# A convolution's running sum moved into a PSUM bank, and two score tiles that share three banks

## The chip, the cores and the metric

The kernel runs on one core of a Trainium2 chip. Time is device microseconds (us) of one execution; the number that counts is the median of three runs. One further execution was recorded by the hardware profiler, and all rows below come from it. PE is the matrix engine (its weight loads are listed as PEld), DVE the vector engine, ACT the scalar engine, POOL the third elementwise engine, SP the engine that issues transfers. SBUF is the working memory. PSUM is the accumulator memory that PE writes to: 8 banks of 512 fp32 columns on each of 128 partitions.

## What is computed

Two transformer-like blocks follow each other, each of two layers, on 512 tokens of width 1024. The change touches only the second block's mixer. It has three branches whose results are concatenated: a Fourier mix, a latent attention of 8 heads, and a depthwise convolution of 31 taps over 256 channels. In the first layer of the block a context of 256 tokens goes through the same mixer; in the second layer only the 512 tokens do, while attention still reads all 768 keys.

```python
def conformer_conv(zg, w_dw, b_dw, ln_g, ln_b, w_pw2):
    a, g = jnp.split(zg, 2, axis=-1)
    u = a * jax.nn.sigmoid(g)
    u = lax.conv_general_dilated(u, w_dw[:, None, :], ...) + b_dw     # 31 taps
    u = jax.nn.silu(layer_norm(u, ln_g, ln_b))
    return u @ w_pw2

def mla_attend(qn, qr, kn, kr, v):
    s = jnp.einsum("bqhd,bkhd->bhqk", qn, kn) + jnp.einsum("bqhr,bkr->bhqk", qr, kr)
    p = jax.nn.softmax(s.astype(jnp.float32) * ATTN_SCALE, axis=-1).astype(v.dtype)
    return jnp.einsum("bhqk,bkhd->bqhd", p, v)
```

## The kernel before

Every product is made of three matmuls (high times high, high times low, low times high part), so that each operand exists as a rounded copy (written by ACT) and a remainder (written by DVE or POOL).

The program is not issued in the order in which the code is written. The functions record operations through proxies, all on line 489 of the kernel, which is why every row of the profile names that line. `Sched.run` then orders them: it steps through a planned time with a cost for each operation (`_cost`) and a flag for operations of DVE and POOL that may not run side by side (`_port`), takes on each engine the ready operation that stands first in priority, and gives out buffers by tag. A tag is a set of slots; an operation that needs a slot waits in the plan until one is free. The instructions are issued in the planned order, each engine works through its own in that order, and semaphores are set between them by a layer below that sees which instruction touches which tile.

The two mixers of the second block are one phase each, `m20` and `m21` in the code. `B2` says how the eight banks are used there: `sc2` holds attention scores, two tiles of 1024 columns, which is four banks; the other four banks are single tiles for everything else. A block of scores has 128 queries by 768 keys, or by 256 keys where the context attends to itself, so a block fills half to three quarters of such a tile.

In `attend` each block of scores is made by a group of matmuls (nine of 256 columns for 768 keys, three for 256), then DVE takes the row minimum (`tensor_reduce`), and ACT the exponential with its sum (`activation`, followed by a small read of the accumulator). PE transposes the exponentials, ACT and DVE split them, PE multiplies them with the values. With 8 heads the first layer has 32 blocks of 768 keys and 16 of 256, the second 32 of 768.

The convolution runs beside all this, as filling. `taps(i, b)` does one block of 128 channels (b) of one stream (i: the tokens or the context). Of the 31 taps 25 run on DVE, as a chain in which each takes the shifted input `cu`, multiplies it with a column of `half` and adds the running sum `a`, a tile of tag `h` in SBUF. The other six (`BESIDE`) are products made by ACT and POOL and summed by POOL into `c`; a last addition of POOL joins the two. `conv_rest` does the normalisation and the closing matmuls. `conv` lays the two channel blocks side by side, one tap of each at a step; `tick` and the loop over `fills` decide how many steps have been recorded by which point of the other work.

Of the kernel before, what the change touches and what calls it, by code (L numbers as in the profile page):

```python
# [12 lines left out]
F32 = mybir.dt.float32  # L13
# [3 lines left out]
ALU = mybir.AluOpType  # L17
AX = mybir.AxisListType

P = 128  # L20
# [23 lines left out]
MIX = 0.5  # L44
WAIT = 1.0
MARGIN = 100
TICK = 3
FREE = 0.2
DMA = 2.0
FSTEP = (20, 18)  # L50
CSTEP = (48, 32)
B2 = {"sc2": 2, "mm tr acc ms": 4}
BESIDE = 6
TAPS = 'AP'
NEARLY = 4
# [470 lines left out]


def _in_psum(x):
    return isinstance(x, View) and x.buf.tag in ("mm", "tr", "acc", "ms", "sc", "sc2")


def _port(eng, name, out, ins):
# [33 lines left out]
def kernel(  # L566
# [30 lines left out]
    sc = Sched(tc)  # L597
    TE, V, S, G, SP = (sc.proxy(e) for e in ("PE", "DVE", "ACT", "POOL", "SP"))
# [22 lines left out]
    def psum(tag="mm", n=T):  # L621
        return sc.alloc(banks.get(tag, tag), n)
# [710 lines left out]
    def mixer2(l, mp, ux, uc):  # L1333
        last = l == L - 1
        NK = T + TC
        SX, SC = (ux[0], ux[1], T), (uc[0], uc[1], TC)
        both = [SX] if last else [SX, SC]
# [33 lines left out]
        def taps(i, b):  # L1371

            u, n, first = convs[i][b], both[i][2], 31 - BESIDE
            a = accs[n, b] = sc.alloc("h", n)
            c = sc.alloc("h", n)
            done = 0
            for j in range(first):
                if j == 0:
                    V.tensor_scalar(out=a, in0=u[:, 0:n], scalar1=wdw(b * 31), scalar2=col(f"bdw{l}", b), op0=ALU.mult, op1=ALU.add)
                else:  # L1380
                    V.scalar_tensor_tensor(out=a, in0=u[:, j:j + n], scalar=wdw(b * 31 + j), in1=a, op0=ALU.mult, op1=ALU.add)
                while done * first < (j + 1) * BESIDE:
                    k = first + done
                    q = t32(n) if done else c
                    if TAPS[done % len(TAPS)] == "A":
                        S.activation(q, u[:, k:k + n], AF.Copy, scale=wdw(b * 31 + k))
                    else:
                        G.tensor_scalar(out=q, in0=u[:, k:k + n], scalar1=wdw(b * 31 + k), scalar2=0.0, op0=ALU.mult, op1=ALU.add)
                    if done:
                        G.tensor_tensor(out=c, in0=c, in1=q, op=ALU.add)  # L1390
                    done += 1
                yield
            G.tensor_tensor(out=a, in0=a, in1=c, op=ALU.add)

        def conv_rest(acc, n):
            xs = [out_split(acc[b], n) for b in range(2)]
# [72 lines left out]
        def fourier(ams):  # L1469

            for s, am in reversed(list(zip(both, ams))):
                n = s[2]
                parity = n // TC
                yf[n] = [operand(n) for f in range(2)]
                for p in range(parity):
                    w = wload(dft_d[(0 if n == T else 2) + p])
                    ps = psum()
                    for f in range(2):
                        o = slice(f * TC, f * TC + TC)
                        for t in range(4):  # L1480
                            x = am[p * 2 + t // 2]
                            a = slice(t % 2 * 256 + f * P, t % 2 * 256 + f * P + P)
                            c = slice(t * TC, t * TC + TC)
                            mm3(ps[:, o], x[0][:, a], x[1][:, a], w[0][:, c], w[1][:, c], t == 0, t == 3)
                        split(*(x.rearrange("p (j b) -> p b j", b=parity)[:, p] for x in yf[n][f]), ps[:, o])
                        yield
# [83 lines left out]
        def block_taps(b):  # L1570
            for i in range(len(both)):
                yield from taps(i, b)

        def conv():
            yield from zip_longest(block_taps(0), block_taps(1))
            for s in both:
                yield from conv_rest([accs[s[2], b] for b in range(2)], s[2])

        convs, yf, yc, accs = [[] for _ in both], {}, {}, {}
        cv, ticks = conv(), [0]  # L1580
# [145 lines left out]
                    v = values(1)  # L1726

        steps = main()
        fills = [(fourier(ams), 4 if last else 6, FSTEP[l]), (cv, (31 - BESIDE + 4) * len(both) - ticks[0], CSTEP[l])]
        done = [0, 0]  # L1730
        for i, _ in enumerate(steps, 1):
            for x, (f, n, span) in enumerate(fills):
# [9 lines left out]
    @contextmanager  # L1742
    def phase(name, shares, slots=()):

        with ExitStack() as st:
            p = pool(name, None, st)
            pp = pool(name + "p", bass.MemoryType.PSUM, st)
            banks.clear()
            sc.here = [tags.split()[0] for tags in shares]
            for tags, n in shares.items():  # L1750
                tag = tags.split()[0]
                banks.update((x, tag) for x in tags.split())
                if tag == "sc2":
                    sc.slots(pp, tag, n, 1024, F32)
                    banks["sc"] = "sc2"
                else:
                    sc.slots(pp, tag, n, 512, F32)
            for tag, n, cols, dt in slots:
                sc.slots(p, tag, n, cols, dt, tag in ("r", "t"))
            yield p  # L1760
            for tag, n in SPARE.get(name[:2], {}).items():
                sc.tags[tag].spare = n
            sc.run()
            sc.drop_extra()
# [264 lines left out]
```

## Time and profile before

| | us |
|---|---|
| median of three runs | 3466.51 (3465.47 to 3468.73) |
| the profiled execution | 3464.11 |
| its span, first to last instruction | 3462.3 |
| PE busy | 3366.1 (97% of the span) |
| DVE busy | 2293.6 (66%) |
| ACT busy | 1458.9 (42%) |
| POOL busy | 795.3 (23%) |

The shares are means over stages that differ. The mixer of the second block's first layer lies at about 1900 to 2200 us of the span, that of the second layer at about 2820 to 3060. In each, projections come first, and then a stretch of attention: from the first score matmul to the last group of them it goes from 2020.70 to 2176.80 in the first layer and from 2931.00 to 3030.70 in the second. A matmul is listed with some 280 ns although one of 256 columns follows the next after about 117 ns, because matmuls overlap; so PE's busy time counts the tail of the last one before a gap as well. In the rows of groups an instruction's mean duration stands in ns behind the busy time, and the idle time before it at the end.

### The profile page before, as it was taken

To read this page: it belongs to the slowest core of one execution; us is meant where nothing else is said; L and a number is where in the kernel's file an instruction comes from. 1 tells how busy PE (TensorE), PEld (TensorE's weight loads), DVE (VectorE), ACT (ScalarE), POOL (GpSimd) and SP (SyncE) were. 2 spreads that over 40 slices of the span, in tenths; PEclk is the share of its full clock that TensorE was granted. 3 is DMA by queue.
4 is the path that set the end of the run, shared out by engine and by line. 5 is a ranking of instruction groups with operands and counts; after the bars stand their busy time and mean duration, and the time that the engine had idled before them with its cause. 6 is when DMAs were issued, how large, how long until landed. Compare 5 with 4: busy or idle time off the path is not lost.

```text
span 3462.3 us, 48309 instructions
## 1 busy us (share of the span) xinstructions
PE 3366.1 (97%) x18565; PEld 2901.3 (84%) x18565; DVE 2293.6 (66%) x4092; ACT 1458.9 (42%) x2751; POOL 795.3 (23%) x710
## 2 busy tenths in 40 slices
PE   8999999999999999999999988999999998999999
PEld 8888888888888888888888876898888887888888
DVE  8888875865388788658654998564443369963334
ACT  5555444322355554443223376441221244843223
POOL 3112323111131032231112443120110235320002
PEclk9999999999999999999999999999999999999999
DMA  3222223543332212236533110223332221123332
GB/s 126 64 71 67 74 67 134 191 168 127 106 101 65 71 61 80 73 134 195 176 128 116 46 37 7 98 80 112 109 109 92 68 81 48 32 79 98 97 96 81
DMA packets 100744, 326.14 MB, mean 94 GB/s; under 512 B 11168, under 2 KB 18336, under 8 KB 100512
## 3 DMA queue, kind: packets, MB, share of 16 engines
q1 hardware_dynamic: 100512, 323.05, 29.0%
q8 instruction: 145, 2.38, 0.3%
q14 instruction: 87, 0.71, 0.1%
HBM read 313.57 MB, written 9.44 MB: 93 GB/s over the span
## 4 chain that ended last, share of the span: by engine, by line
PE 84%; DVE 10%; ACT 3%; issue 2%; POOL 1%; DMA 0%; SPq 0%; DVEq 0%; ACTq 0%; POOLq 0%
PE mm L489 78%; PE sc L489 4%; DVE r L489 3%; DVE h L489 2%; DVE s L489 2%; PE acc L489 2%; DVE t L489 1%; ACT r L489 1%; DVE w L489 1%; ACT e L489 1%; ACT t L489 0%; DMA raw<-in_win_dram 0%; ACT w L489 0%; POOL t L489 0%; POOL x L489 0%
## 5 line engine op out<-in xcount | busy, mean ns | idle before, releaser
L489 PE MATMUL mm<-r,w 128*128 128x512 f32 (+2 forms) x12044 | 2521.2, 360 | 17.7 <-DVE w L489 7.5
L489 PEld LDWEIGHTS mm<-r,w 128*128 128x128 f32 (+1 forms) x12044 | 2009.0, 189 | 347.6 <-DVE w L489 11.0
L489 DVE TENSOR_TENSOR w<-raw,w 128x1024 fp32r<-128x1024 f32 (+2 forms) x466 | 588.2, 1270 | 639.6 <-issue 327.8
L489 ACT ACTIVATE w<-raw 128x1024 fp32r<-128x1024 f32 (+1 forms) x466 | 483.5, 1047 | 1035.1 <-PE mm L489 946.8
L489 ACT ACTIVATE e<-sc,s 128x512 f32<-128x512 f32 (+2 forms) x208 | 153.4, 740 | 99.6 <-DVE s L489 94.7
L489 POOL TENSOR_TENSOR x<-t,x 128x512 fp32r<-128x512 f32 (+1 forms) x58 | 83.0, 1434 | 409.1 <-ACT x L489 397.5
L489 PE MATMUL mm<-rc,w 128*128 128x256 f32 x768 | 166.1, 281 | 0.0
L489 PEld LDWEIGHTS mm<-rc,w 128*128 128x128 f32 x768 | 139.8, 189 | 20.2
L489 DVE TENSOR_REDUCE s<-sc 128x1 f32<-128x512 f32 (+2 forms) x208 | 151.4, 741 | 7.6 <-PE sc L489 7.1
L489 POOL TENSOR_TENSOR t<-t,t 128x512 f32<-128x512 f32 (+2 forms) x70 | 89.0, 1273 | 237.5 <-DVE t L489 200.3
L489 PE MATMUL mm<-r,r 128*128 128x256 f32 (+1 forms) x588 | 118.8, 333 | 8.1 <-DVE r L489 6.8
L489 ACT ACTIVATE t<-mm 128x512 f32<-128x512 f32 (+4 forms) x126 | 68.0, 540 | 135.0 <-PE mm L489 129.9
L489 DVE SCALAR_TENSOR_TENSOR h<-cu,half,h 128x512 f32<-128x512 f32 (+1 forms) x144 | 116.4, 819 | 0.5
L489 PE MATMUL mm<-sums 128*128 128x256 f32 x757 | 107.2, 291 | 9.7 <-DVE sums L489 6.4
L489 DVE TENSOR_TENSOR r<-mm,r 128x256 fp32r<-128x256 f32 (+1 forms) x266 | 105.6, 433 | 14.3 <-ACT r L489 12.4
L489 ACT ACTIVATE r<-mm 128x256 fp32r<-128x256 f32 (+1 forms) x272 | 94.8, 401 | 44.5 <-PE mm L489 41.3
L489 PEld LDWEIGHTS mm<-sums 128*128 128x128 f32 x757 | 101.2, 198 | 13.2 <-DVE sums L489 6.6
L489 ACT ACTIVATE r<-t 128x512 fp32r<-128x512 f32 (+3 forms) x141 | 83.1, 597 | 68.8 <-DVE t L489 55.9
L489 PEld LDWEIGHTS mm<-r,r 128*128 128x128 f32 x588 | 90.8, 193 | 23.4 <-DVE r L489 8.4
L489 DVE TENSOR_TENSOR r<-t,r 128x512 fp32r<-128x512 f32 (+2 forms) x134 | 105.4, 794 | 7.5 <-ACT r L489 6.3
L489 PE MATMUL mm<-w,r 128*128 128x256 f32 x704 | 102.4, 285 | 4.9 <-DVE w L489 3.1
L489 PEld LDWEIGHTS mm<-w,r 128*128 128x128 f32 x704 | 91.5, 190 | 7.4 <-DVE w L489 3.5
(636 smaller groups left out, 4358.8 us busy)
## 6 DMA issues: line engine op xcount, KB each, us to landing
raw<-in_wm_dram SPq DMA_DIRECT2D x256, 512.0 KB, 3.5
raw<-in_win_dram SPq DMA_DIRECT2D x134, 512.0 KB, 3.6
mraw<-in_wmod_dram SPq DMA_DIRECT2D x64, 512.0 KB, 4.4
raw<-in_wmod_dram SPq DMA_DIRECT2D x32, 512.0 KB, 3.5
raw<-in_wbr_dram SPq DMA_DIRECT2D x24, 512.0 KB, 3.5
raw<-in_wout_dram SPq DMA_DIRECT2D x16, 512.0 KB, 4.0
raw<-in_wo_dram SPq DMA_DIRECT2D x16, 512.0 KB, 3.5
kept<-h SPq DMA_DIRECT2D x24, 256.0 KB, 3.2
```

Source lines behind the costliest of these rows:

```text
L489: getattr(self.engines[eng], name)(*[_real(x) for x in a], **{n: _real(x) for n, x in k.items()})
```

## The change

The running sum of the DVE taps lies in a PSUM bank of its own (tag `cv`, one slot) in place of SBUF; the bank is named as PSUM to the planner, which then no longer takes these taps for operations that keep POOL waiting. The last addition of a chain goes from POOL to DVE, from PSUM and SBUF to a tile of tag `h`. To free the bank, the two score tiles have 768 columns each and are cut from one tile of 1536 columns, three banks; the first covers the first bank and half of the second, the other the rest. Since there is one slot for a running sum, the channel blocks are done one behind the other. A step is now one tap, so the number of steps is doubled in `TICK` and in `fills`.

```diff
-TICK = 3
+TICK = 6
...
-B2 = {"sc2": 2, "mm tr acc ms": 4}
+B2 = {"sc2": 2, "mm tr acc ms": 4, "cv": 1}
...
-    return isinstance(x, View) and x.buf.tag in ("mm", "tr", "acc", "ms", "sc", "sc2")
+    return isinstance(x, View) and x.buf.tag in ("mm", "tr", "acc", "ms", "sc", "sc2", "cv")
...
             u, n, first = convs[i][b], both[i][2], 31 - BESIDE
-            a = accs[n, b] = sc.alloc("h", n)
-            c = sc.alloc("h", n)
+            a, c = psum("cv", n), sc.alloc("h", n)
...
-            G.tensor_tensor(out=a, in0=a, in1=c, op=ALU.add)
+            accs[n, b] = sc.alloc("h", n)
+            V.tensor_tensor(out=accs[n, b], in0=c, in1=a, op=ALU.add)
...
         def conv():
-            yield from zip_longest(block_taps(0), block_taps(1))
+            for b in range(2):
+                yield from block_taps(b)
...
-        fills = [(fourier(ams), 4 if last else 6, FSTEP[l]), (cv, (31 - BESIDE + 4) * len(both) - ticks[0], CSTEP[l])]
+        fills = [(fourier(ams), 4 if last else 6, FSTEP[l]), (cv, (2 * (31 - BESIDE) + 4) * len(both) - ticks[0], CSTEP[l])]
...
                 if tag == "sc2":
-                    sc.slots(pp, tag, n, 1024, F32)
+                    t = pp.tile([P, n * 768], F32, tag=tag, name=tag)
+                    sc.tags[tag] = Tag([t[:, i * 768:(i + 1) * 768] for i in range(n)], 0)
```

DVE, first layer, start of the convolution, before. `cu5120` and `cu5121` are the padded inputs of the two channel blocks of the tokens, `cu2560` that of the context, `h5` and `h1` running sums, `w` and `raw` weights.

```order
L489 SCALAR_TENSOR_TENSOR h5_144<-cu5120_14461,half_14465,h5_144 128x512 [waits DVE_49] x2
L489 TENSOR_TENSOR w0_102<-raw0_108,w2_104 128x1024 [waits DMAHW2_49,PE_49,Activation_49]
L489 SCALAR_TENSOR_TENSOR cu2560_14463<-t5_120,mm0_14453 128x256
L489 TENSOR_TENSOR w5_107<-raw2_110,w5_107 128x8x32 [waits DMAHW4_49,Activation_49]
L489 SCALAR_TENSOR_TENSOR h5_144<-cu5120_14461,half_14465,h5_144 128x512 [waits DVE_49]
L489 TENSOR_SCALAR h1_140<-cu2560_14463,half_14465,vec_148 128x256 [waits DVE_49]
L489 SCALAR_TENSOR_TENSOR h5_144<-cu5120_14461,half_14465,h5_144 128x512 [waits DVE_49]
L489 TENSOR_TENSOR w3_105<-raw1_109,w4_106 128x1024 [waits DMAHW3_49,PE_49]
L489 SCALAR_TENSOR_TENSOR h5_144<-cu5120_14461,half_14465,h5_144 128x512 [waits DVE_49] x6
```

The same place in the changed kernel; `cv0` is the running sum in PSUM.

```order
L489 SCALAR_TENSOR_TENSOR cv0_14456<-cu5120_14461,half_14465,cv0_14456 128x512 [waits DVE_49] x2
L489 TENSOR_TENSOR w0_102<-raw0_108,w2_104 128x1024 [waits DMAHW2_49,PE_49,Activation_49]
L489 SCALAR_TENSOR_TENSOR cu2560_14463<-t5_120,mm0_14452 128x256
L489 SCALAR_TENSOR_TENSOR cv0_14456<-cu5120_14461,half_14465,cv0_14456 128x512 [waits DVE_49]
L489 TENSOR_TENSOR w5_107<-raw2_110,w5_107 128x8x32 [waits DMAHW4_49,Activation_49]
L489 SCALAR_TENSOR_TENSOR cv0_14456<-cu5120_14461,half_14465,cv0_14456 128x512 [waits DVE_49] x6
L489 TENSOR_TENSOR w3_105<-raw1_109,w4_106 128x1024 [waits DMAHW3_49,PE_49]
L489 SCALAR_TENSOR_TENSOR cv0_14456<-cu5120_14461,half_14465,cv0_14456 128x512 [waits DVE_49] x9
```

The first chain runs through in long rows, and the context's chain, which had begun beside it, comes after it. At the first score matmul of the first layer 43 DVE taps are left in place of 60: 19 of 512 columns and 24 of 256, where there were 12 and 48.

DVE, second layer, the fifth and sixth reduction of attention before. `sc20` and `sc21` are the two score tiles, `e` and `s` belong to the exponentials, `r`, `mm` and `t` to the split of transposed tiles.

```order
L489 TENSOR_REDUCE s10_133<-sc20_22061 128x1 [waits PE_49]
L489 TENSOR_TENSOR r14_76<-mm2_22065,r6_68 128x2x128 [waits PE_49,Activation_49]
L489 TENSOR_TENSOR r39_101<-mm2_22065,r17_79 128x2x128
L489 TENSOR_TENSOR r27_89<-mm0_22063,r30_92 128x2x128 [waits Activation_49]
L489 SCALAR_TENSOR_TENSOR h5_144<-cu5121_22072,half_22075,h5_144 128x512 [waits DVE_49]
L489 RECIPROCAL s8_131<-s0_123 128x1 [waits Activation_49]
L489 TENSOR_REDUCE s5_128<-sc21_22062 128x1
L489 SCALAR_TENSOR_TENSOR h4_143<-cu5120_22071,half_22075,h4_143 128x512 [waits DVE_49]
```

The fifth to the seventh in the changed kernel, where `sc2` is the one tile of 1536 columns:

```order
L489 TENSOR_REDUCE s4_127<-sc2_22066 128x1 [waits PE_49]
L489 TENSOR_TENSOR r3_65<-mm1_22068,r19_81 128x2x128 [waits Activation_49]
L489 TENSOR_REDUCE s6_129<-sc2_22066 128x1 [waits Activation_49]
L489 RECIPROCAL s0_123<-s1_124 128x1
L489 TENSOR_TENSOR r22_84<-mm2_22069,r33_95 128x2x128 [waits PE_49,Activation_49]
L489 TENSOR_TENSOR r14_76<-mm2_22069,r2_64 128x2x128
L489 TENSOR_TENSOR r3_65<-mm1_22068,r19_81 128x2x128 [waits Activation_49]
L489 TENSOR_REDUCE s2_125<-sc2_22066 128x1 [waits Activation_49]
```

Two of the three reductions wait for ACT: what they wait for is the exponential of the other half of the tile. Before, no reduction of these two phases waits for ACT; now 14 do in the first layer and 10 in the second. In the same way 15 and 9 exponentials wait for a group of score matmuls of the other half, and 23 and 16 such groups wait for a reduction or an exponential of the other half. Before, each waits for its own tile only.

PE, second layer, around the sixth group of score matmuls before:

```order
L489 MATMUL mm2_22065<-ident_150,e0_22068 128x128 [waits Activation_49]
L489 MATMUL mm2_22065<-ident_150,e0_22068 128x128 x3
L489 MATMUL sc21_22062<-k1h_22080,q1h_22081 128x256
L489 MATMUL sc21_22062<-k1l_22082,q1h_22081 128x256
L489 MATMUL sc21_22062<-k1h_22080,q1l_22083 128x256
```

and in the changed kernel around the seventh, which writes the first half of the tile:

```order
L489 MATMUL mm2_22069<-ident_150,e0_22073 128x128 [waits DVE_49]
L489 MATMUL mm2_22069<-ident_150,e0_22073 128x128 x3
L489 MATMUL mm1_22068<-ident_150,e0_22073 128x128 [waits DVE_49]
L489 MATMUL mm1_22068<-ident_150,e0_22073 128x128
L489 MATMUL sc2_22066<-k1h_22085,q1h_22086 128x256 [waits DVE_49]
```

The wait for DVE on the last row counts to the reduction of the second half (`s6`, the sixth, shown above). The tile is thus used by one engine at a time, in the order in which the program lists the accesses, whichever half they touch. In the second layer these are 96 (32 groups, 32 reductions, 32 exponentials), with 75 changes of engine between them, 23 of them away from PE.

## Rows read from the trace of the kernel before

**Rows 1.** Chain of waits of the whole span: shares by engine.

```profile
PE 84%; DVE 10%; ACT 3%; issue 2%; POOL 1%; DMA 0%; SPq 0%; DVEq 0%; ACTq 0%; POOLq 0%
```

**Rows 2.** Busy times by stretch: projections and attention, first layer, then second.

```profile
core 0: us, PE busy (x) PEld busy (x) DVE busy (x) ACT busy (x) POOL busy (x), PEclk, DMA share, GB/s
1900.00:2020.70 120.70, 113.25 (x687) 99.38 (x687) 108.70 (x198) 54.33 (x107) 58.84 (x50) 0.97 0.18 58
2020.70:2176.80 156.10, 130.91 (x936) 116.64 (x934) 141.05 (x331) 115.33 (x297) 61.40 (x67) 0.96 0.04 13
2820.00:2931.00 111.00, 98.17 (x562) 84.02 (x562) 102.89 (x175) 49.13 (x91) 56.90 (x47) 0.95 0.21 67
2931.00:3030.70 99.70, 93.09 (x724) 87.08 (x723) 95.39 (x208) 82.79 (x202) 38.78 (x36) 1.00 0.10 33
```

**Rows 3.** Waits of PE in attention (total, times, longest): first layer, then second.

```profile
PE mm L489 <- DVE r L489: 10.8, 18, 1.4
PE sc L489 <- ACT e L489: 7.1, 8, 1.8
...
PE mm L489 <- DVE r L489: 3.9, 8, 1.1
```

**Rows 4.** DVE taps by shape, in the four stretches of group 2.

```profile
L489 DVE SCALAR_TENSOR_TENSOR h<-cu,half,h 128x512 f32<-128x512 f32 x36 | 33.7, 942 | 0.3
L489 DVE SCALAR_TENSOR_TENSOR h<-cu,half,h 128x512 f32<-128x512 f32 x13 | 11.4, 899 | 0.0
L489 DVE SCALAR_TENSOR_TENSOR h<-cu,half,h 128x256 f32<-128x256 f32 x48 | 25.1, 541 | 0.1
L489 DVE SCALAR_TENSOR_TENSOR h<-cu,half,h 128x512 f32<-128x512 f32 x31 | 30.9, 1005 | 0.1
L489 DVE SCALAR_TENSOR_TENSOR h<-cu,half,h 128x512 f32<-128x512 f32 x17 | 16.1, 949 | 0.0
```

**Rows 5.** Timeline (start, duration): POOL additions, a tap beside them, a tap alone.

```profile
1920.46 7.10 POOL L489 TENSOR_TENSOR h<-h,t 128x512 f32<-128x512 f32 x4
1924.63 1.78 DVE L489 SCALAR_TENSOR_TENSOR h<-cu,half,h 128x512 f32<-128x512 f32 x1
...
2944.63 0.74 DVE L489 SCALAR_TENSOR_TENSOR h<-cu,half,h 128x512 f32<-128x512 f32 x1
```

**Rows 6.** DVE with one operand in PSUM, first projections and second attention.

```profile
L489 DVE SCALAR_TENSOR_TENSOR cu<-t,mm 128x512 f32<-128x512 f32 x2 | 1.4, 688 | 3.8 <-ACT t L489 2.2 <-PE mm L489 1.6
...
L489 DVE TENSOR_TENSOR r<-mm,r 128x256 fp32r<-128x256 f32 x86 | 31.6, 415 | 1.8 <-ACT r L489 1.5
```

**Rows 7.** Timeline of score tiles in the second layer's attention.

```profile
2942.78 0.94 DVE L489 TENSOR_REDUCE s<-sc 128x1 f32<-128x768 f32 x1
2943.76 0.90 ACT L489 ACTIVATE e<-sc,s 128x768 f32<-128x768 f32 x1
2944.56 0.19 ACT L489 ACTIVATION_READ_ACCUMULATOR e<-sc,s 128x1 f32 x1
...
2948.54 0.93 DVE L489 TENSOR_REDUCE s<-sc 128x1 f32<-128x768 f32 x1
...
2948.85 0.36 PE L489 MATMUL sc<-k1h,q1h 128*128 128x256 f32 x1
```

**Rows 8.** Timeline: first and ninth matmul of a group of scores.

```profile
2931.04 0.28 PE L489 MATMUL sc<-k0h,q0h 128*128 128x256 f32 x1
...
2931.98 0.28 PE L489 MATMUL sc<-k0h,q0l 128*128 128x256 f32 x1
```

**Rows 9.** Row minimum and exponential in attention, by shape.

```profile
L489 DVE TENSOR_REDUCE s<-sc 128x1 f32<-128x768 f32 x30 | 28.1, 946 | 0.0
...
L489 DVE TENSOR_REDUCE s<-sc 128x1 f32<-128x256 f32 x15 | 6.2, 411 | 0.0
...
L489 ACT ACTIVATE e<-sc,s 128x768 f32<-128x768 f32 x30 | 27.1, 907 | 4.9 <-DVE s L489 4.5
```

## Prediction

> **What bounds the kernel now.** I read the chain of waits first: PE holds 84% of it, DVE 10%, ACT 3% and POOL 1% [rows 1]. Then the busy times by stretch, since the change acts in four stretches only [rows 2]. PE is idle there for 120.70 - 113.25 = 7.5 us (projections, first layer), 156.10 - 130.91 = 25.2 us (attention, first layer), 111.00 - 98.17 = 12.8 us (projections, second layer) and 99.70 - 93.09 = 6.6 us (attention, second layer). So 52 us is all that an engine beside PE can give back, and in the second layer's attention there is hardly anything to win and much to lose. DVE stands close behind PE in every stretch: 108.7 of 120.7, 141 of 156, 103 of 111, 95 of 99.7. Then the waits of PE in attention: 10.8 us for remainders `r` by DVE and 7.1 us for exponentials that still hold a score tile in the first layer, 3.9 us for `r` in the second [rows 3]. DVE is the engine to relieve, the score tiles the place to be careful with.
>
> **The taps.** The 144 DVE taps take 33.7 + 11.4 + 25.1 + 30.9 + 16.1 = 117.2 us in the four stretches [rows 4]. One of 512 columns takes 0.94 to 1.00 us in the projections, but 0.74 where POOL is still; beside POOL's additions a single tap took 1.78, and four such additions 7.10 us [rows 5]. A tap with its sum in PSUM isn't in the trace. The nearest rows have one operand in PSUM: 0.688 us for 512 columns, 0.415 for 256 [rows 6]. The dear end is the contended tap of today, 1.0 us, in case the shifted input in SBUF alone is enough to collide with POOL. I take 0.68 and 0.415, since those rows stand in the same stretches, beside the same POOL.
>
> [...]
>
> By stretch, with the counts of the new order: before the first score matmul of the first layer there are now 29 taps of 512 columns and 24 of 256, 29 × 0.68 + 24 × 0.415 = 29.7 us in place of 33.7, so 4.0 less. In its attention 19 and 24 remain, 12.9 + 10.0 = 22.9 in place of 36.5, so 13.6 less. In the second layer 35 before attention, 23.8 for 30.9, 7.1 less, and 13 in it, 8.8 for 16.1, 7.3 less. The six last additions come to DVE from POOL: 4 × 0.68 + 2 × 0.415 = 3.5 us more. DVE is relieved of about 28 us.
>
> Little of that is time in the projections: PE's idle time is 7.5 and 12.8 us there, and part of it is other waits than for DVE. I take -2 and -4 us; the bounds are 0 and -4, 0 and -7. In attention the relief goes into the sum below. That the two channel blocks stand in a row costs nothing as I see it: each tap already waits for one of its own engine only, and a chain from one `h` shows rows of 0.74. POOL has 59 of 121 us at most to do, so that its six products keep up.
>
> **The score tiles.** This is the part that I think decides. The two tiles were two objects, each with its own waits. Now they are slices of one, and the new order shows that a wait is set for whatever touched the tile last, in either half. An access of PE, DVE or ACT in one half therefore waits for the one listed before it in the other. Before, writing one tile goes on while the other is read: in the trace a reduction runs from 2948.54 to 2949.47, and PE starts a group into the other tile at 2948.85 [rows 7]. That group would have to wait 0.6 us. 23 groups in the first layer and 16 in the second wait in this way now.
>
> What the chain of accesses costs if it runs end to end, second layer: a group of nine matmuls takes 0.94 + 0.12 = 1.05 us [rows 8], a reduction 0.95 [rows 9], an exponential 0.99 up to the end of its accumulator read (2943.76 to 2944.75) [rows 7]. 32 × (1.05 + 0.95 + 0.99) = 95.7. Of 75 changes of engine 23 lead away from PE, at 0.22 us, since the last matmul's result lies about 0.16 us behind its place in the row and a hand-over of 0.06 follows; the other 52 take 0.04 to 0.09 (a reduction ends at 2943.72, the exponential starts at 2943.76 [rows 7]): 5.1 + 3.6 = 8.7. Less 3 for the accesses behind the last group: 101.4 us. The stretch takes 99.7 now [rows 2], so the chain alone, which knows nothing of other work, is already longer.
>
> It won't run without gaps. Between two accesses PE has at one place 92 other matmuls listed, 11 us at 0.12, of which only 3.4 is covered by accesses on other engines; that adds about 7.5, and smaller places 1.8: 110.7. And DVE is busy 95 of 100 us before the relief, about 85 after, with instructions of 0.41 and 0.68: a reduction that becomes ready finds DVE in the middle of one, about 0.2 us each, 6 us over 32. ACT is in a like place at 0.16 us, 5 us. That is 121.7. Against 99.7 the loss is 11 to 22 us; I take +18, above the middle, because a late group also delays the matmuls of `mm` that are queued behind it on PE, and those hold up ACT and DVE, which split them. The relief of 5.9 us of DVE (7.3 less two additions) is in this. Bounds: +8, if the planner's order leaves other work between most accesses, and +25.
>
> First layer: 32 × 2.99 + 16 × (0.35 + 0.41 + 0.56) = 95.7 + 21.1 = 116.8, with three matmuls, the reduction of 256 columns [rows 9] and an exponential of 256 estimated from the wide one. 127 changes of engine, 39 of them away from PE: 39 × 0.22 + 88 × 0.07 = 14.8. Together 131.6; about 7 for places where PE has more to do than the accesses cover, and 18 for late reductions and exponentials by the same shares: 156. The stretch takes 156.1 now, with much of the same lateness in it, since PE waits for DVE and ACT anyway [rows 3], and DVE is relieved of 13.6 less 2.2 us there. I take 0, bounds -12 and +12.
>
> PE's granted clock is 0.96 in the first layer's attention, where PE is busy 84%, and 1.00 in the second, with 93% [rows 2]. [...] I take +2 for it, 0 to +5.
>
> **Sum.** -2 - 4 + 0 + 18 + 2 = +14 us. The profiled execution took 3464.1, so 3478; the median of the runs lies 2.4 above it: 3480.
>
> **Rivals.** *Faster, by DVE's relief.* The accesses of the two halves alternate with enough other work for PE between them that the new waits are hidden, and DVE's 28 us count where PE waits for `r`: 10.8 and 3.9 us [rows 3], and 4 and 7 in the projections. For it: these waits are the largest of PE in the stretches. Against it: the new order puts the waits at the first matmul of a group, and all matmuls behind it are held. With about half of these 26 us won and none lost, -13: 3453. It decides from the point where the tile waits cost less than 6 us in both layers.
>
> *They cancel.* Both as in the forecast, but the second layer loses only 8 and the first wins 3 by DVE's relief: -2 - 4 - 3 + 8 = -1: 3466.
>
> *Dear taps, on the slower side.* The sum in PSUM costs as much as the contended tap of today, 1.0 us for 512 columns and 0.54 for 256. Then 96 × 0.32 + 48 × 0.125 = 37 us of DVE come on top of my estimate, the relief turns into 8 us more, and in attention the reductions are later still. The forecast loses its -6, and the first layer's attention goes to about +10: 14 + 6 + 10 = +30, 3497. For it: beside POOL a single tap took 1.78 us, and one of its three operands stays in SBUF [rows 5]. Against it: one operand in PSUM, 0.688 [rows 6].
>
> *The half tiles don't wait for each other.* If the waits could tell the halves apart, this would be the faster rival; the order shows that they don't, so it has no chance of its own.
>
> **How the numbers follow.** Tile waits decide: 0.5. Faster by relief: 0.2. They cancel: 0.2. Dear taps: 0.1. A measurement can't tell 0.2%, 7 us, from no change. Slower by more than that: 0.5 + 0.1 = 0.6; within: 0.2; faster: 0.2. The forecast's own range is 3471 to 3496 (second layer +8 to +25, the rest by about half its bounds). The range for 8 in 10 goes to 3450 below, where the faster rival lies, and to 3505 above, past the dear taps.
>
> **What would show it.** Right: the second layer's attention takes 108 to 125 us, with PE waiting for DVE's `s` and ACT's `e` at `sc` rows, some 16 times, 10 us or more together; in the first layer 23 such waits. Taps `cv<-cu,half,cv` of 512 columns at 0.65 to 0.75, whether POOL runs or not. Projections 2 to 4 us shorter. Wrong: the second attention within 3 us of 99.7, or taps near 1 us, or a gain in the projections of more than 6 us, which would mean that DVE had set their pace.

## Result: 28 us slower, and the profile after

The changed kernel takes 3493.5 us (median of 4 runs, 3490.36 to 3496.19), the kernel before in the same comparison 3465.99. The ratio is 1.008, 95% interval 1.0062 to 1.0097. The profiled execution took 3490.36 us, 26.25 more than that of before, with a span of 3488.6.

Six stretches take up this difference. The marks between them are the first score matmul and the start of the last group of them in each of the two mixers, and the first addition of an output (`h<-mm,mod0x,h`) behind the first mixer. Each time is in us of one profiled execution. Executions reach us 1900 with up to 4 us between them, though the code up to there is the same; where that matters below, the first `cu<-t,mm` (the padded input of the convolution) serves as a mark.

| stretch | before | changed | difference |
|---|---|---|---|
| projections, first layer (from 1900) | 120.7 | 115.2 | -5.5 |
| attention, first layer | 156.1 | 159.3 | +3.2 |
| from the last scores to the first output addition | 27.6 | 37.1 | +9.5 |
| from there to the second layer's first scores | 726.7 | 720.9 | -5.8 |
| attention, second layer | 99.7 | 123.6 | +23.9 |
| the rest | 431.6 | 432.5 | +0.9 |

These are the busy times of the changed kernel by stretch, in the columns of [rows 2], with the end of the first mixer as third row:

```profile
1900.00:2015.15 115.15, 109.09 (x670) 96.05 (x671) 106.44 (x218) 52.86 (x106) 58.02 (x55) 0.99 0.18 60
2015.15:2174.40 159.25, 126.37 (x912) 112.20 (x911) 128.19 (x302) 114.34 (x291) 48.10 (x55) 0.98 0.04 13
2174.40:2211.50 37.10, 30.32 (x183) 25.60 (x182) 22.43 (x57) 15.24 (x36) 6.79 (x7) 0.95 0.43 142
2820.00:2932.50 112.50, 100.39 (x579) 85.78 (x578) 100.43 (x199) 50.37 (x95) 54.65 (x50) 0.95 0.22 76
2932.50:3056.10 123.60, 99.08 (x732) 87.97 (x730) 92.45 (x199) 84.45 (x205) 32.73 (x33) 1.00 0.09 31
```

In the second layer's attention PE is idle for 123.60 - 99.08 = 24.5 us, where it was 6.6. DVE and ACT have about the same work in it as before, so no engine got fuller; all of them wait. The third row stands against this one of before, with 46 matmuls fewer:

```profile
2176.80:2204.40 27.60, 23.48 (x137) 20.18 (x138) 18.86 (x47) 12.46 (x30) 2.62 (x4) 0.94 0.57 191
```

Not all of these matmuls are work. Where its plan leaves PE idle, the planner puts in products of a constant tile with itself (`warm` in `Sched.run`, the rows `mm<-sums`), which nobody reads. The profile counts them as busy. In that stretch there were 26 before, and there are 57 now:

```profile
L489 PE MATMUL mm<-sums 128*128 128x256 f32 x26 | 5.1, 341 | 2.0 <-DVE t L489 2.0
...
L489 PE MATMUL mm<-sums 128*128 128x256 f32 x57 | 8.6, 294 | 0.4 <-DVE t L489 0.2 <-DVE s L489 0.2
```

So 31 of the 46 are such fillers and 15 are work. At 0.117 us each the 31 are an estimated 3.6 us, and PE's idle time in the stretch grew from 4.1 to 6.8: some 6 of its 9.5 us are time for which PE had too little work.

The waits of PE in the changed kernel (total, times, longest), first layer's attention and behind the dots the second's, answer to [rows 3]:

```profile
PE sc L489 <- ACT e L489: 10.8, 12, 1.6
PE sc L489 <- DVE s L489: 6.9, 7, 1.4
PE mm L489 <- DVE r L489: 5.4, 9, 1.1
...
PE sc L489 <- ACT e L489: 6.0, 7, 1.2
PE mm L489 <- DVE r L489: 5.8, 8, 1.3
PE sc L489 <- DVE s L489: 4.8, 5, 1.6
```

Before, the score tiles cost PE 7.1 us in the first layer and none in the second; now it is 17.7 and 10.8. The wait for `s`, the row minimum, is new: a group of matmuls has no reason to wait for a minimum of its own half, since the exponential of that half came later. The timeline of the second layer shows how one wait makes the next (start, duration, and in brackets the idle time before with what ended it):

```profile
2980.45 0.39 PE L489 MATMUL sc<-k1h,q1h 128*128 128x256 f32 x1 [0.15 <-DVE s L489]
2981.87 0.90 ACT L489 ACTIVATE e<-sc,s 128x768 f32<-128x768 f32 x1 [1.09 <-PE sc L489]
2982.89 0.96 DVE L489 TENSOR_REDUCE s<-sc 128x1 f32<-128x768 f32 x1 [1.59 <-ACT e L489]
2983.91 0.39 PE L489 MATMUL sc<-k1h,q1h 128*128 128x256 f32 x1 [1.47 <-DVE s L489]
```

PE writes one half; ACT, whose exponential reads the other half and was ready, idles 1.09 us until those matmuls are done; DVE's reduction of the half just written idles 1.59 until that exponential is done; PE's next group, for the half that ACT has just left, idles 1.47 until the reduction is done. Three engines take turns on one tile.

The taps with their sum in PSUM, first layer's projections (two shapes) and attention (two), then the second layer's two stretches:

```profile
L489 DVE SCALAR_TENSOR_TENSOR cv<-cu,half,cv 128x512 f32<-128x512 f32 x29 | 21.8, 753 | 0.7
L489 DVE SCALAR_TENSOR_TENSOR cv<-cu,half,cv 128x256 f32<-128x256 f32 x24 | 11.7, 486 | 0.6
...
L489 DVE SCALAR_TENSOR_TENSOR cv<-cu,half,cv 128x512 f32<-128x512 f32 x20 | 14.9, 743 | 0.0
L489 DVE SCALAR_TENSOR_TENSOR cv<-cu,half,cv 128x256 f32<-128x256 f32 x24 | 11.5, 478 | 0.1
...
L489 DVE SCALAR_TENSOR_TENSOR cv<-cu,half,cv 128x512 f32<-128x512 f32 x35 | 26.2, 749 | 0.4
...
L489 DVE SCALAR_TENSOR_TENSOR cv<-cu,half,cv 128x512 f32<-128x512 f32 x13 | 9.7, 743 | 0.1
```

One of 512 columns takes 743 to 753 ns in every stretch, where it took 899 to 1005 in SBUF [rows 4].

### The profile page after: what moved, and what is told of

It is laid out like the page before. It is cut to its first block, busy times and chain, and to the rows that moved or that the text cites. A ratio compares the mean times of both kernels' runs of the same rounds, so it can differ in the third digit from the quotient of the medians.

```text
span 3488.6 us, 48262 instructions
## 1 busy us (share of the span) xinstructions
PE 3364.7 (96%) x18541; PEld 2895.0 (83%) x18541; DVE 2271.1 (65%) x4098; ACT 1459.9 (42%) x2751; POOL 774.1 (22%) x704
## 4 chain that ended last, share of the span: by engine, by line
PE 85%; DVE 9%; ACT 3%; issue 2%; DMA 0%; POOL 0%; SPq 0%; DVEq 0%; ACTq 0%; POOLq 0%
PE mm L489 79%; PE sc L489 5%; DVE s L489 2%; DVE r L489 2%; PE acc L489 2%; DVE t L489 1%; ACT e L489 1%; DVE w L489 1%; DVE h L489 1%; ACT r L489 1%; DVE cv L489 1%; ACT t L489 0%; ACT w L489 0%; DVE x L489 0%; DMA raw<-in_win_dram 0%
## 5 line engine op out<-in xcount | busy, mean ns | idle before, releaser
L489 DVE TENSOR_REDUCE s<-sc 128x1 f32<-128x512 f32 (+2 forms) x208 | 151.7, 743 | 33.2 <-PE sc L489 17.7
L489 PE MATMUL mm<-r,r 128*128 128x256 f32 (+1 forms) x588 | 117.8, 333 | 13.5 <-DVE r L489 11.5
L489 DVE SCALAR_TENSOR_TENSOR cv<-cu,half,cv 128x512 f32<-128x512 f32 (+1 forms) x144 | 95.0, 659 | 2.0
```

The source lines that it names most:

```text
L489: getattr(self.engines[eng], name)(*[_real(x) for x in a], **{n: _real(x) for n, x in k.items()})
```

## Experiments

All were timed in five rounds beside the kernel before, whose median lay between 3464.1 and 3465.3.

**One part alone: the shared tile.** The kernel before, with this edit in the pool only. Its instructions keep their order on every engine.

```diff
-                    sc.slots(pp, tag, n, 1024, F32)
+                    t = pp.tile([P, n * 768], F32, tag=tag, name=tag)
+                    sc.tags[tag] = Tag([t[:, i * 768:(i + 1) * 768] for i in range(n)], 0)
```

> The kernel before, with the two score tiles cut from one tile of 1536 columns and nothing else; its instructions stand in the same order on every engine, only the waits between the two halves are added. Theory (the waits of one half for the other make the loss): the second layer's attention goes from 99.7 to 115 to 127 us, the first layer's mixer gets 8 to 15 us longer, the whole 24 to 36 us longer, 3490 to 3502. Rival (the loss comes with the new order of the convolution and with its sum in PSUM): within 5 us of before.

Measured: 3502.76 us, ratio 1.0114 (1.0101 to 1.0128). That is 37 us, more than the whole change costs and just above the expected range. The two attention stretches:

```profile
2022.26:2200.14 177.88, 138.61 (x936) 120.30 (x934) 142.99 (x331) 116.64 (x297) 59.95 (x67) 0.93 0.04 11
...
2953.91:3069.69 115.78, 96.50 (x724) 87.14 (x723) 97.42 (x209) 84.31 (x204) 38.27 (x37) 1.00 0.10 33
```

The first grew by 21.8, far more than the 8 to 15 expected there, the second by 16.1; together 37.9. The first has the same 936 matmuls as before, 14.1 us more idle time of PE and 7.7 more busy time at a mean granted clock of 0.93 in place of 0.96 (before, it was 0.50 from 2077.1 to 2080.4 and from 2135.2 to 2145.2, and 1.00 in the rest of the stretch). The waits of PE in it:

```profile
PE mm L489 <- DVE r L489: 10.6, 18, 1.2
PE sc L489 <- ACT e L489: 10.3, 12, 2.3
PE sc L489 <- DVE s L489: 7.0, 11, 1.4
PE mm L489 <- ACT e L489: 6.5, 5, 1.9
```

Against 7.1 and 3.1 for the second and fourth of these before, that is 10 us more at the scores and 3 at the transposes of late exponentials. The theory of the waits holds, though not its size in the first layer, and the rival falls.

**Waits or the bank in the middle.** The same, with 2048 columns, so that no bank holds parts of both halves.

```diff
-                    sc.slots(pp, tag, n, 1024, F32)
+                    t = pp.tile([P, n * 1024], F32, tag=tag, name=tag)
+                    sc.tags[tag] = Tag([t[:, i * 1024:(i + 1) * 1024] for i in range(n)], 0)
```

> The kernel before, with the two score tiles cut from one tile of 2048 columns, so that each half has two banks of its own and only the waits are shared. Theory of the waits: the same time as with three banks, within 3 us. Rival (what costs is that both halves lie in one bank, where one engine writes while another reads): over 8 us less than with three banks, near before.

Measured: 3505.69 us, 1.0121 (1.0107 to 1.0134), 3 us from the one with three banks. The loss comes with the one tile, not with where it lies.

**One part alone: the channel blocks in a row,** the sum in SBUF, two score tiles.

```diff
-TICK = 3
+TICK = 6
...
-            yield from zip_longest(block_taps(0), block_taps(1))
+            for b in range(2):
+                yield from block_taps(b)
...
-        fills = [..., (cv, (31 - BESIDE + 4) * len(both) - ticks[0], CSTEP[l])]
+        fills = [..., (cv, (2 * (31 - BESIDE) + 4) * len(both) - ticks[0], CSTEP[l])]
```

> The kernel before, with the channel blocks of the convolution one behind the other and a step of one tap; the sum stays in SBUF, the score tiles stay two. Theory of the waits: within 5 us of before. Rival (the order of the convolution makes the end of the first layer's mixer later): 6 to 12 us more, with the stretch from the last scores to the first output addition longer by as much.

Measured: 3470.95 us, 1.0016 (1.0008 to 1.0025), 6 us more. The stretch at the end of the first mixer, the second row, grew by 10.5, as the rival said, but the attention before it shrank by 7.4:

```profile
2020.56:2169.29 148.73, 127.77 (x912) 113.17 (x911) 139.16 (x310) 111.58 (x287) 60.81 (x63) 0.98 0.04 10
2169.29:2207.44 38.15, 30.82 (x183) 26.43 (x182) 22.96 (x61) 16.17 (x39) 5.35 (x6) 0.91 0.45 152
```

The matmul counts are 912 and 183, as in the changed kernel, where there were 936 and 137. Most of what moved is filler: 22 fell to 10 in attention, and 26 rose to 58 behind it. Some 14 more are work that now stands behind the last scores.

```profile
L489 PE MATMUL mm<-sums 128*128 128x256 f32 x58 | 8.7, 294 | 0.6 <-DVE r L489 0.5 <-DVE t L489 0.2
```

What the longer end goes with is the last tap. With the chains side by side (before, the two experiments above, and the kernel before with nothing but the mark, further below) it starts 28 to 39 us ahead of the last scores of the first layer, and the stretch behind them takes 26 to 28 us. With the chains in a row it starts 8 to 16 us ahead of them, in the changed kernel 2158.9 for 2174.4, and the stretch takes 33 to 38 us. The one exception in a row, the single slot below, has its last tap 86 us ahead, and the stretch takes 14. That the late normalisation behind the last tap makes the stretch long was not tried by itself. The net cost of the row is 3.1 us in the first mixer and some 5 in the second, whose end after the last scores is later.

**Undone in one layer.** The changed kernel, the second layer with two tiles of their own; that leaves three banks for everything else there.

```diff
-        with phase(f"m2{l}", B2,
+        with phase(f"m2{l}", B2 if l == 0 else {"sc2": 2, "mm tr acc ms": 3, "cv": 1},
...
+                    if name == "m20":
                         t = pp.tile([P, n * 768], F32, tag=tag, name=tag)
                         sc.tags[tag] = Tag([t[:, i * 768:(i + 1) * 768] for i in range(n)], 0)
+                    else:
+                        sc.slots(pp, tag, n, 1024, F32)
```

> The changed kernel, with two score tiles of their own (four banks) in the second layer, where three banks are left for everything else; the first layer is unchanged. Theory of the waits: the second layer's attention falls from 123.6 to 96 to 108 us, the whole to 3469 to 3478. Rival (the sum in PSUM or the order makes that stretch long): it stays above 118 us, the whole at 3488 or more.

Measured: 3479.26 us, 1.0038 (1.0024 to 1.0052). The stretch is back at 102.5 us, and PE's waits for score tiles in it have gone from 10.8 to 0.5:

```profile
2936.32:3038.86 102.54, 91.40 (x703) 84.13 (x702) 87.94 (x188) 79.62 (x195) 30.04 (x31) 1.00 0.11 37
```

Part of that is work that only moved: 29 matmuls that are no fillers left the stretch and 30 came behind it. The whole is 1 us above what was expected, for 7 us come back behind the last scores (439.7 for 432.5 in the last stretch), where PE also waits 3.2 us for remainders and 1.2 for `t` with three banks, and 0.7 for remainders with four. So the shared tile's price in the second layer of the changed kernel is some 14 us, 3493.5 - 3479.3, net of what the three banks cost elsewhere. The first layer was not tried so.

**The sum back in SBUF,** everything else as changed (this is the first and the third experiment together).

> The changed kernel with its shared score tile and its channel blocks in a row, but the running sum back in SBUF and the last addition on POOL. Theory (three parts that add up: +37 for the shared tile, +6 for the blocks in a row, and -15 for the sum in PSUM): 3500 to 3514. Rival (the sum in PSUM gives nothing, the new order alone softens the tile's waits): 3489 to 3497, as the changed kernel.

Measured: 3521.16 us, 1.0163 (1.0149 to 1.0177), above both expectations; the rival falls, and the three parts don't simply add up. The shared tile costs more in the order with the blocks in a row, 3521.2 - 3471.0 = 50 us, than in that of before, and the sum in PSUM is worth 28 us. In the first layer's attention the steps are 148.7 us with the blocks in a row, 172.7 with the shared tile as well, and 159.3 with the sum in PSUM:

```profile
2023.21:2195.94 172.73, 133.84 (x916) 116.10 (x914) 139.05 (x311) 112.77 (x287) 59.04 (x62) 0.96 0.03 9
```

**Where do these 28 us come from?** The planner is told by the name of a bank that a tap may run beside POOL, so the change does two things at once. First the sum in PSUM without telling:

```diff
-    return isinstance(x, View) and x.buf.tag in ("mm", "tr", "acc", "ms", "sc", "sc2", "cv")
+    return isinstance(x, View) and x.buf.tag in ("mm", "tr", "acc", "ms", "sc", "sc2")
```

> The changed kernel, except that the planner is not told that the running sum lies in PSUM: it still keeps taps and POOL's operations apart in its plan, and the order is that of a sum in SBUF. Theory (the gain of the sum in PSUM is that DVE's taps no longer run at half pace beside POOL): 3489 to 3500, near the changed kernel. Rival (the gain comes from the other order that the planner makes): 3510 to 3521, near the kernel with the sum in SBUF.

Measured: 3519.65 us, 1.0156 (1.0142 to 1.017): nothing gained, so the theory falls that the taps' pace on DVE is the gain. The taps do take 743 to 750 ns in it. Its first projections, and behind them the same stretch with the sum in SBUF:

```profile
1900.00:2022.90 122.90, 115.39 (x694) 101.24 (x694) 95.47 (x207) 55.18 (x110) 53.26 (x52) 0.96 0.20 63
```

```profile
1900.00:2023.21 123.21, 115.70 (x707) 101.52 (x706) 107.84 (x212) 56.10 (x113) 59.86 (x54) 0.97 0.20 67
```

DVE has 12.4 us less to do and the stretch is 0.3 us shorter; counted from the first `cu<-t,mm` (1919.4 and 1921.0) it is 1.3 us longer. Then the order without the cheap taps: a sum in an `h` tile that is marked as PSUM for the planner. The order is nearly that of the changed kernel; some rows differ, as there is more than one slot for a sum.

```diff
-            a, c = psum("cv", n), sc.alloc("h", n)
+            a, c = sc.alloc("h", n), sc.alloc("h", n)
+            a.buf.told = True
...
-    return isinstance(x, View) and x.buf.tag in (...)
+    return isinstance(x, View) and (x.buf.told or x.buf.tag in (...))
```

> [...] Theory after the last run (the 28 us between sum in SBUF and sum in PSUM come from the order that the planner makes when it no longer keeps taps and POOL apart): 3489 to 3500. Rival (order and cheap taps are needed together: in this order slow taps delay what was planned tightly): 3508 to 3525.

Measured: 3516.83 us, 1.0151 (1.0138 to 1.0165). My theory, that the order alone does it, falls as well. With the shared tile the four cases are:

| | planner not told | told |
|---|---|---|
| sum in SBUF | 3521.2 | 3516.8 |
| sum in PSUM | 3519.7 | 3493.5 |

Either alone gives 1.5 and 4.4 us, which the scatter of these runs (intervals of 5 us to either side) can't tell from nothing; both together give 28. In this fourth case the first projections show what lacks: DVE needs 121.5 us in them, and the stretch is 6 us longer than with the old order, 8 from the first `cu<-t,mm`.

```profile
1900.00:2029.11 129.11, 113.43 (x679) 98.11 (x679) 121.50 (x224) 53.85 (x107) 62.76 (x55) 0.97 0.17 58
```

And the kernel before with nothing but the mark on its sums:

> The kernel before, with sums, score tiles and channel blocks as they were; only the planner is told that a tap may run beside POOL. Theory of the order (the plan kept taps and POOL apart for more than the chip's collision is worth): 3446 to 3459. Rival (order and cheap taps together): 3462 to 3480.

Measured: 3465.62 us, 1.0002 (0.9993 to 1.0011). Without cheap taps the freer order gives nothing there either.

**One slot that the planner knows of.**

```diff
-B2 = {"sc2": 2, "mm tr acc ms": 4, "cv": 1}
+B2 = {"sc2": 1, "mm tr acc ms": 5, "cv": 1}
...
-                    t = pp.tile([P, n * 768], F32, tag=tag, name=tag)
-                    sc.tags[tag] = Tag([t[:, i * 768:(i + 1) * 768] for i in range(n)], 0)
+                    sc.slots(pp, tag, n, 1024, F32)
```

> The changed kernel with a single score tile in two banks, and five banks for everything else, so that the planner knows that one block of scores is in work at a time and orders the rest around it. Theory (the run from matmuls to minimum to exponential is serial, known or not): the second layer's attention takes 105 to 125 us, the whole 3480 to 3500. Rival (the loss comes from waits that the planner did not know, and goes when it does): second attention under 103 us, the whole under 3475.

Measured: 3506.36 us, 1.0121 (1.0108 to 1.0135), above what either expected. The second attention takes 143.0 us with 864 matmuls in it in place of 732, and PE waits there at the transposes of exponentials:

```profile
PE mm L489 <- ACT e L489: 22.3, 24, 1.7
...
L489 PE MATMUL mm<-sums 128*128 128x256 f32 x106 | 16.0, 283 | 0.6 <-DVE r L489 0.6
```

106 of these matmuls are fillers, where the changed kernel has 6: the planner saw that PE would run dry and had nothing better to put there. A planner that knows of the serial use doesn't hide it, even with a fifth bank for the rest.

**A version that keeps two tiles and takes the cheap taps.** Until attention starts nobody needs the score tiles. The first channel block's sums go into one of them, the second's stay in SBUF; the banks are those of before, the blocks in a row.

```diff
+FIRST = lambda i, b: b == 0
...
-            a = accs[n, b] = sc.alloc("h", n)
-            c = sc.alloc("h", n)
+            a, c = psum("sc", n) if FIRST(i, b) else sc.alloc("h", n), sc.alloc("h", n)
+            accs[n, b] = a
...
-            G.tensor_tensor(out=a, in0=a, in1=c, op=ALU.add)
+            if FIRST(i, b):
+                accs[n, b] = sc.alloc("h", n)
+                V.tensor_tensor(out=accs[n, b], in0=c, in1=a, op=ALU.add)
+            else:
+                G.tensor_tensor(out=a, in0=a, in1=c, op=ALU.add)
```

> The kernel before with two score tiles of their own, the channel blocks in a row, and the running sum of the first channel block (tokens, then context) in a score tile that is not needed yet; the second block's sum stays in SBUF. Theory (DVE's relief beside POOL is worth 3 to 5 us in each projection stretch, the row costs 6): 3459 to 3468. Rival (the relief counts only inside attention, where DVE is late): 3468 to 3473, as with the blocks in a row alone.

Measured: 3456.08 us, 0.9973 (0.9962 to 0.9984), 8.6 us below before and faster than both kernels. The gain was above expectation, and its place was not where I had put it. The attention of the first layer fell by 19.7 to 136.4 us, with 915 matmuls and a clock of 1.00. The stretch behind its last scores gave back 7.9, the stretch up to the second layer's scores lost another 5.4, and its attention gave back 5.3. The first projections are 4.5 longer from us 1900 on, but the first `cu<-t,mm` came 3.0 later in this execution (1920.6 for 1917.6), so that 1.5 is left for the change. Why so much came back in that attention was not tried.

```profile
2025.17:2161.62 136.45, 121.02 (x915) 110.52 (x914) 128.41 (x294) 110.48 (x287) 53.76 (x58) 1.00 0.05 15
2161.62:2197.14 35.52, 29.24 (x174) 25.36 (x173) 22.27 (x56) 15.97 (x40) 5.99 (x6) 0.90 0.45 149
```

The same with tokens first (`for i ...: for b in range(2): yield from taps(i, b)`) and only one chain of each layer in a score tile:

> As the one before, but the order of the chains is tokens first (both channel blocks), then context, and only the first chain of each layer has its sum in a score tile. Theory (relief in the projections, and the tokens' normalisation is no longer late): 3457 to 3466. Rival (what makes the end late is that the chains stand in a row, whichever comes first): 3466 to 3473.

Measured: 3457.39 us, 0.9979 (0.997 to 0.9988). And the version before it with `TICK = 8`:

> The version with the first channel block's sum in a score tile, with 8 in place of 6 steps of the convolution at each point of the projections, so that more of the second block's taps are recorded before attention. Theory (DVE has room in the projections since its first chains no longer collide with POOL, and is short in attention): 3448 to 3456. Rival (priority in the plan hardly follows these steps, or DVE then delays the projections): 3456 to 3464.

Measured: 3455.91 us, 0.9976 (0.9966 to 0.9985), on the border between the two expectations. The three can't be told apart.

## Why the prediction was right, and where it was not

The forecast was +14 us for the profiled execution, slower by the waits between the halves; it became +26.3, near twice that, with the median inside the forecast's own range. The mechanism is shown by the first, second and fourth experiment. The nearness is partly luck: terms that were mis-sized or left out partly cancel. Term by term:

- **Second layer's attention, +18, and +2 for the clock.** Measured +23.9. The number asked for was 108 to 125 us with 10 us or more of waits at the scores: 123.6 and 10.8, in 12 waits where some 16 were expected. The timeline above shows late reductions and exponentials of the kind that was worked out; how much each adds was not measured. No run shows the +2 for the clock: it stayed at 1.00 in this stretch while PE was busy for 80%, and in the first experiment while PE was busy for 83%.
- **First layer's attention, 0.** Measured +3.2, but by large terms that cancel. The waits alone cost 21.8 there, as the first experiment shows; in the new order they cost 24, the row of blocks gives 7.4 and the sum in PSUM 13.5 back. I had worked out 156 us, 131.6 for the chain on the tile and the rest for lateness, compared it with a stretch of 156.1 and concluded that nothing is lost; yet of before's 156.1 a part is idle time for other reasons, such as 10.8 us for remainders, and that wait stayed at 10.6 when the chain on the tile was added. The chain of one resource is a lower bound, not a forecast; the measured times here, 177.9 without DVE's relief and 159.3 with it, lie above what I made of it.
- **Blocks in a row, nothing.** This is the step that failed: "costs nothing as I see it". I had looked at the waits of a tap and not at what the order does to the work behind the chains. The stretch behind the last scores got 9.5 longer in the changed kernel and 10.5 in the third experiment, where 7.4 came back in attention; the net price of that experiment is 6 us in all, and the waits cost 50 in the new order where they cost 37 in the old. No term of the sum stood for that stretch, and its 9.5 us are the largest part of the 12 us that the forecast was short.
- **Projections, -2 and -4.** Measured -5.5 and -5.8; direction right, size too small: the first lies outside its bound of -4, the second inside -7. Each also came close to the 6 us that I had named as a sign of being wrong, and the two together are above it. The bounds were taken from PE's idle time of 7.5 and 12.8 us, and "52 us is all that an engine beside PE can give back" was wrong for the same reason: PE's busy time holds the fillers, 13 and 98 of them in these two stretches, 134 in all four, an estimated 16 us at 0.117 each. In the changed kernel the first has none; from the first `cu<-t,mm` to the scores of the second layer 79 fell to 40, and that part shrank by 5.6, from 86.7 us to 81.1. Fewer fillers alone don't do it: the told sum in SBUF has 37 there and takes 87.8. Of the 17 matmuls that the first has fewer [rows 2], 13 are fillers. The reason for the gain wasn't the one that I gave either: cheaper taps alone give the first projections nothing that stands out of the scatter between executions, and only an order made for them brings the rest.
- **Price of a tap, 0.68 and 0.415.** Measured 0.743 to 0.753 and 0.478 to 0.486, whether POOL works or not. The row that came nearest was not the one I took: a tap alone in SBUF took 0.74 [rows 5]. The taps sum up to 95.8 us, not 85.2, and DVE's relief from them is 21 us, not 32. The rival of dear taps is out, though its time, 3497, was nearest to the measured one.

The fillers in the second layer's projections before, by the mark of [rows 2]:

```profile
L489 PE MATMUL mm<-sums 128*128 128x256 f32 x98 | 13.0, 283 | 0.0
```

What stays open: why the waits cost 13 us more in the order with the blocks in a row. In the profiled executions 7 of it lie in the two attention stretches (24 and 21 for 22 and 16). There 20 reductions wait for ACT, where 13 do in the order of before with the shared tile, and none with two tiles. Whether these 7 waits make the difference was not tried. Open too is what exactly holds up the end of the first mixer, as said above.

## What to carry to other kernels

Two buffers that are slices of one tile were one buffer here to whatever sets the waits, at 37 us in the first experiment; before joining them, list the accesses of all engines in program order and count the changes of engine. A chain that this makes is a lower bound on the stretch; here, where it was as long as the stretch of the second layer (101 for 99.7 us), the stretch grew to 123.6. Count as busy only what is work: a planner's fillers look busy in a profile, and hide both what there is to win and what an order loses. And where a planner orders the work, an edit has two effects, on the chip and on the plan, and each can be worthless without the other: change them one at a time before giving the gain to either.

## What the runs showed of the hardware that was not expected

A tap of 512 columns with its sum in PSUM takes the same time beside POOL as without it, 743 to 753 ns over the four stretches, although its other operand still comes from SBUF; in SBUF it took 899 to 1005. Single instructions say it more sharply: in the changed kernel the 40 taps with no POOL instruction beside them took 745 ns on average and the 31 that lay wholly beside POOL 752; before, 50 alone took 742 and 15 beside POOL 1380. The subtractions that make remainders show no price of a source in PSUM either: with no POOL instruction beside them, 512 columns took 685 ns on average from PSUM (`r<-mm,r`) and 685 from SBUF (`r<-t,r`), in the kernel before. Halves that share a bank and halves with two banks each gave the same time, 3502.8 and 3505.7, but here the waits keep engines from using both at once, so this says nothing on simultaneous use. The mean granted clock in the first attention was 0.93 with PE busy 78% of it (shared tile alone), and 0.98 with 79% (changed kernel): the busy share of the stretch alone doesn't tell it.
